# RWKV-7 recurrence: 32x32 triangular inverses by substitution on 16-blocks and 32x32 products

## The chip, the cores and the metric

The kernel runs on one core of a Trainium2 chip. The metric is the device time of one execution in microseconds (us). A core has TensorE (PE in the profile; PEld is its weight load), VectorE (DVE), ScalarE (ACT), GpSimd (POOL), SyncE (SP, which issues nearly all DMAs here) and 16 DMA engines.

## The reference

A network of four blocks on 512 tokens of width 1024 in f32: banded attention, an MLP, an RWKV-7 mixer with its MLP, and a block with an S5 and an LRU recurrence. Only the mixer's scan matters here. It runs for 16 heads of 64 channels, once forwards and once backwards over the tokens:

```python
def rwkv7_scan(r, w, k, v, kk, a):
    def step(state, inp):
        r_t, w_t, k_t, v_t, kk_t, a_t = inp
        sa = jnp.einsum('bhvk,bhk->bhv', state, -kk_t)
        state = (state * w_t[:, :, None, :] + sa[..., None] * (kk_t * a_t)[:, :, None, :]
                 + v_t[..., None] * k_t[:, :, None, :])
        return state, jnp.einsum('bhvk,bhk->bhv', state, r_t)
    ...
```

Written for a chunk of 64 tokens at a time, the steps inside a chunk become products with the inverse of a 64x64 triangular matrix with ones on its diagonal, and only the state is carried from chunk to chunk.

## The kernel before

The mixer's projections come first, then the recurrence, then the output projection. The recurrence works on 8 pairs of heads, `p` = 0 to 7. A pair has 8 chunks of 64 tokens, 2 directions `d` and 2 heads `hp`, so 32 triangular 64x64 matrices. Each is made of two 32x32 triangular blocks on the diagonal and one full block beside them. A pair therefore has 64 triangular 32x32 blocks; `g` = 2d + half numbers the four kinds, `x` = 0 to 15 the sixteen blocks of a kind (chunk and head).

Ten streams of instructions are written as Python generators, each run for p = 0 to 7:

- `front` and `half` (one per direction) load and form the decay-scaled operands `ar` and `bk` of a pair, mostly on DVE and ACT.
- `scores` multiplies them on PE, masks the products on DVE into the tile `at`, four tiles `at` a pair, and stores the triangular blocks to the DRAM scratch `nd_s`. Blocks of direction 1 are transposed on DVE first (line 1627).
- `inverse` loads a pair's 64 blocks back, so that a partition holds a whole 32x32 block (`N`). Each block stands on two partitions, one for the even rows of its inverse (`X`), one for the odd. Then 30 columns are eliminated one after the other, each by a product and a sum on DVE (lines 1656 and 1659, which the profile shows under the helper's line 1298), and `X` goes to the DRAM scratch `xd_s`.
- `early` makes `uv` from v. `merge` loads the inverses as 32x32 blocks on partitions (`yz`), transposes them on DVE (line 1700), and joins two 32-blocks into a 64-block by two rounds of 32 products of 32x32 on PE (lines 1715 and 1725), into the tile `tt`.
- `mid` multiplies with `tt` and makes, for each chunk, the matrix `m` by which the state changes. `chain` carries the state: 8 steps a pair, each a product on PE into `cp` and four ACT instructions that write the next state `ss` (line 1831). `post` normalises, and its end must be issued before the chain of the next pair begins.

The function `weave` merges the streams into one order for each engine: at every turn it takes the stream whose next instruction could start first by a model of costs and waits (2.2 us for any DMA), and of several with the same start the one whose operands were ready first. This order is fixed in the program, so an instruction that waits holds up all that stands behind it on its engine. Conditions keep the streams together. `scores` of a pair may go on only when the chain of two pairs earlier has made enough steps, because nine tiles `at` are there:

```python
yield lambda: min(done["side", 0], done["side", 1]) > 2 * p + i // 2 and done["step"] >= 2 * (4 * p + i - 9) + 2
```

`inverse` starts when the fourth tile `at` of its pair is there, `merge` when `inverse` and `early` are.

Of the kernel before, what the change touches and what calls it, by code (L numbers as in the profile page):

```python
# [24 lines left out]
class Net:  # L25
# [200 lines left out]
    def bank(self):  # L226
        return self.ps.tile([128, 512], F32, name="mm", tag="mm")
# [1063 lines left out]
    def rwkv(self, g_pre, mu_p, mu_n, w_r, w_k, w_v, w_o, k_k, k_a, r_k, gn_w, gn_b, w0, w1, w2, a0, a1, a2,  # L1291
# [4 lines left out]
        nc, tc = self.nc, self.tc  # L1296
        V, G = nc.vector, nc.gpsimd
# [29 lines left out]
        with ExitStack() as c0:  # L1327
            prm = self.pool(c0, "rprm", side="right")

            with ExitStack() as c1:  # L1330
# [3 lines left out]
                for n, lst in enumerate(((("mp", mu_p, 48), ("mn", mu_n, 48)),  # L1334
# [4 lines left out]
                    o = 0  # L1339
# [93 lines left out]
            with ExitStack() as c1:  # L1433
# [34 lines left out]

                selr = sh.tile([128, 16], F32, name="selr")
# [132 lines left out]
                def scores(p, st):  # L1602


                    nt_ = T2("nt", 1)[:, :S].rearrange("p (a b) -> p a b", b=32)
                    for i in range(4):
# [36 lines left out]
                def inverse(p, st):  # L1643

                    yield lambda: done["pre"] > p
                    N = sh.tile([128, 32, 32], F32, name="N", tag="N")
                    X = sh.tile([128, 16, 32], F32, name="X", tag="X")
# [3 lines left out]
                    yield DV, N, X  # L1651
                    xt = sh.tile([128, 240], F32, name="xt_", tag="xt_")
                    for j in range(1, 31):
                        m, n = (j + 1) // 2, 31 - j
                        t = xt[:, :m * n].rearrange("p (i c) -> p i c", c=n)
                        TT(V, t, X[:, 0:m, j].unsqueeze(2).to_broadcast([128, m, n]),
                           N[:, j, j + 1:32].unsqueeze(1).to_broadcast([128, m, n]), M)
                        yield DV, xt
                        TT(V, X[:, 0:m, j + 1:32], X[:, 0:m, j + 1:32], t, AD)
# [28 lines left out]
                def merge(p, st):  # L1688

                    yield lambda: done["inverse"] > p and done["early"] > p  # L1690
                    yz = sh.tile([128, 32, 32], F32, name="yz", tag="yz")
                    yb, zb = yz[:, 0:16], yz[:, 16:32]
                    t3 = tts[p % 2].rearrange("p c h t -> p (c h) t")
                    for g in (2, 3, 0, 1):
                        s_ = xd_d[p, 16 * g:16 * g + 16].rearrange("x (s t) -> s x t", t=32)
# [11 lines left out]
                    mx, rsb = yb, zb  # L1707
                    b = bank().rearrange("p (x t) -> p x t", t=32)
                    for i in range(4):
                        if i % 2 == 0:  # L1710
                            yield PE, st["at", i], mx
                        for x in range(4 * i, 4 * i + 4):
                            for d in range(2):
                                o = 32 + 32 * d
                                MM(b[Q((1, 2)[d] if x % 2 else 3 * d), x, :], st["at", i][Q(3 * d), x // 2 % 2, x % 2, 2 * d, o:o + 32], mx[Q(3 * d), x, :], True, True)
# [5 lines left out]
                    for x in range(16):  # L1721
                        if x % 8 == 0:
                            yield PE, rsb, mx
                        for d in range(2):
                            MM(b[Q(1 + d if x % 2 else 3 * d), x, :], rsb[Q(1 + d), x, :], mx[Q(1 + d), x, :], True, True)
# [337 lines left out]
```

## Time and profile before

| what | value |
|---|---|
| median of 3 runs | 2375.42 us (2374.48 to 2377.2) |
| the profiled execution | 2374.26 us, its span 2372.5 us |
| PE busy | 2148.4 us (91%), 14218 instructions |
| DVE busy | 1350.9 us (57%), 2862 instructions |
| ACT busy | 1084.0 us (46%), 1958 instructions |
| recurrence, from its first masked scores to its last state | 872 to 1376 us of the span |
| in it: PE, DVE, ACT busy | 400.37, 353.61, 322.46 us of 504 |
| in it: mean granted clock of PE | 0.83 of full speed |

The shares of the whole span mix the recurrence with projections in which PE is busy nearly all the time. What the change is worth has to be read from the recurrence alone. The profiled execution is 1.2 us below the median; 1.8 us of it lie outside the span.

### The profile page before, as it was taken

The page shows a single profiled execution, that of the slowest core. Times are in us where ns is not written, and L with a number is a line of the kernel's source. Part 1 is how long each engine was busy: PE and PEld are TensorE (multiplying, and loading weights), DVE is VectorE, ACT ScalarE, POOL GpSimd, SP SyncE. Part 2 cuts the span into 40 slices and gives each one's busy share as a digit, 9 for nine tenths or more (in the row PEclk, how much of TensorE's full clock was granted, in tenths as well). Part 3 has the DMA queues.
Part 4 walks back from the last instruction along what each step waited for, and adds up shares of the span by engine and source line. Part 5 has one row for each costly group of instructions (what it writes and reads, how often), then busy time and mean ns, then how long its engine had stood idle before and what let it go on. Part 6 is the DMA issues. An engine that isn't in the chain of part 4 may idle for free. (4 is left out here: it accounts for less than half of the span.)

```text
span 2372.5 us, 36431 instructions
## 1 busy us (share of the span) xinstructions
PE 2148.4 (91%) x14218; PEld 1737.5 (73%) x14218; DVE 1350.9 (57%) x2862; ACT 1084.0 (46%) x1958; POOL 82.7 (3%) x121
## 2 busy tenths in 40 slices
PE   8998999999978965788888779999999999999998
PEld 6777788888756854667666658888787877788877
DVE  4556542333479568487867446287655657732353
ACT  4555353342356454567665645342333444532232
POOL 0000000000000001011111000000000000000000
PEclk9999999999979985788889989999999989899999
DMA  5311233233332423233323153234244454233341
GB/s 170 102 54 53 80 107 92 86 107 97 99 103 63 146 65 74 43 65 67 75 44 72 49 173 105 89 109 124 97 134 128 143 133 115 66 90 100 104 142 54
DMA packets 352375, 226.54 MB, mean 95 GB/s; under 512 B 114799, under 2 KB 306315, under 8 KB 352203
## 3 DMA queue, kind: packets, MB, share of 16 engines
q1 hardware_dynamic: 350762, 218.97, 32.8%
q10 hardware_dynamic: 1440, 5.24, 0.6%
q8 instruction: 112, 1.84, 0.3%
q14 instruction: 61, 0.49, 0.1%
HBM read 193.94 MB, written 27.07 MB: 93 GB/s over the span
## 5 line engine op out<-in xcount | busy, mean ns | idle before, releaser
L160 ACT ACTIVATE whi<-raw 128x1024 fp32r<-128x1024 f32 x228 | 239.6, 1052 | 603.0 <-PE mm L223 318.2
L161 DVE TENSOR_TENSOR wlo<-raw,whi 128x1024 fp32r<-128x1024 f32 x228 | 276.3, 1214 | 385.8 <-ACT whi L160 383.0
L222 PE MATMUL mm<-uth,whi 128*128 128x512 f32 (+1 forms) x1088 | 411.7, 380 | 1.7 <-ACT uth L196 1.7
L223 PE MATMUL mm<-utl,whi 128*128 128x512 f32 (+1 forms) x1088 | 406.0, 374 | 5.3 <-DVE utl L197 5.3
L224 PE MATMUL mm<-uth,wlo 128*128 128x512 f32 (+1 forms) x1088 | 406.2, 374 | 0.0
L223 PEld LDWEIGHTS mm<-utl,whi 128*128 128x128 f32 x1088 | 208.1, 191 | 42.9 <-DVE utl L197 6.6
L222 PEld LDWEIGHTS mm<-uth,whi 128*128 128x128 f32 x1088 | 207.8, 192 | 40.5 <-ACT uth L196 2.9
L224 PEld LDWEIGHTS mm<-uth,wlo 128*128 128x128 f32 x1088 | 208.0, 191 | 37.1 <-issue 1.1
L224 PE MATMUL mm<-whi,hl 128*128 128x512 f32 x512 | 200.6, 394 | 0.0
L222 PE MATMUL mm<-whi,hh 128*128 128x512 f32 x512 | 200.5, 394 | 0.0
L223 PE MATMUL mm<-wlo,hh 128*128 128x512 f32 x512 | 199.9, 393 | 0.0
L224 PEld LDWEIGHTS mm<-whi,hl 128*128 128x128 f32 x512 | 96.3, 188 | 22.0 <-issue 0.2
L223 PEld LDWEIGHTS mm<-wlo,hh 128*128 128x128 f32 x512 | 96.3, 188 | 21.7
L222 PEld LDWEIGHTS mm<-whi,hh 128*128 128x128 f32 x512 | 96.3, 188 | 21.4 <-issue 0.4
L1302 PE MATMUL mb<-ar,bk 64*128 64x128 f32 x512 | 85.4, 330 | 16.1 <-DVE ar L1298 13.8
L223 PE MATMUL mm<-mx,whi 128*128 128x512 f32 x224 | 91.3, 407 | 4.5 <-DVE mx L1289 4.4
L222 PE MATMUL mm<-whi,uth 128*128 128x512 f32 x224 | 88.5, 401 | 6.7 <-ACT whi L160 6.4
L222 PE MATMUL mm<-mx,whi 128*128 128x512 f32 x224 | 87.3, 410 | 7.2 <-ACT mx L1288 6.2
L1302 PEld LDWEIGHTS mb<-ar,bk 64*128 64x128 f32 x512 | 72.6, 227 | 24.6 <-issue 15.5
L224 PE MATMUL mm<-mx,wlo 128*128 128x512 f32 x224 | 90.0, 402 | 0.0
L224 PE MATMUL mm<-whi,utl 128*128 128x512 f32 x224 | 88.5, 398 | 0.0
L223 PE MATMUL mm<-wlo,uth 128*128 128x512 f32 x224 | 88.0, 396 | 0.0
(534 smaller groups left out, 3887.9 us busy)
## 6 DMA issues: line engine op xcount, KB each, us to landing
raw<-in_mlp_w_dram SPq DMA_DIRECT2D x128, 512.0 KB, 4.1
raw<-in_w_in_dram SPq DMA_DIRECT2D x44, 512.0 KB, 3.8
raw<-in_attn_w_in_dram SPq DMA_DIRECT2D x18, 512.0 KB, 4.2
gbt<-in_norm_g_dram ACTq DMA_DIRECT2D x8, 512.0 KB
raw<-in_attn_w_out_dram SPq DMA_DIRECT2D x8, 512.0 KB
raw<-in_rk_w_k_dram SPq DMA_DIRECT2D x8, 512.0 KB, 4.4
h_s<-h SPq DMA_DIRECT2D x8, 512.0 KB, 2.7
raw<-in_rk_w_v_dram SPq DMA_DIRECT2D x8, 512.0 KB
```

Of the source, the lines that this page charges most:

```text
L160: nc.scalar.activation(out=hi[:, :n], in_=raw[:, :n], func=AF.Copy)
L161: nc.vector.tensor_tensor(out=lo[:, :n], in0=raw[:, :n], in1=hi[:, :n].bitcast(F32), op=ALU.subtract)
L222: mm(out, lhsT=lhs[0], rhs=rhs[0], start=start, stop=False)
L223: mm(out, lhsT=lhs[0], rhs=rhs[1], start=False, stop=False)
L224: mm(out, lhsT=lhs[1], rhs=rhs[0], start=False, stop=stop)
L1302: MM = lambda o, l, r, a, b: nc.tensor.matmul(o, lhsT=l, rhs=r, start=a, stop=b)
```

## The change

`inverse` no longer eliminates 30 columns of a 32x32 block. A partition now holds one of the two 16x16 triangular blocks on the diagonal of a 32-block: 64 blocks of 32 make 128 of 16, one to a partition, and 14 columns are eliminated in place in `X`. Direction 1 comes in untransposed (`XL`), and one DVE copy turns it round inside each partition. `merge` loads these inverses as 32x32 blocks with zeros beside the diagonal (`yd`), transposes them (`zd`), and makes the 32-blocks on PE: 64 products of 32x32, a mask on DVE (`v1`, with the constant `off`), then 4 products of 32x512 with the identity and 64 products of 32x32 summed on them. From there on it goes as before, except that the operands lie the other way round, which drops two ACT copies.

```diff
+                X, XL, yd, zd = (sh.tile([128, 16, 32], F32, name=n) for n in ("X", "XL", "yd", "zd"))
+                for t in (X, XL, yd):
+                    G.memset(t, 0.0)
...
 def scores(p, st):
-                        yield DV, at
                         for g in (2, 3, 0, 1):
-                            d = g // 2
-                            e = 64 * d + 32 * (g % 2)
-                            s_ = at[Q(g), :, :, 2 * d, e:e + 32].rearrange("p j h t -> p (j h) t")
-                            if g >= 2:
-                                V.transpose(out=nt_[Q(g), 4 * i:4 * i + 4], in_=s_)
-                                s_ = nt_[Q(g), 4 * i:4 * i + 4]
+                            s_ = at[Q(g), :, :, 2 * (g // 2), diag(g)].rearrange("p j h t -> p (j h) t")
...
 def inverse(p, st):
-                    for e in range(2):
-                        nc.sync.dma_start(out=N[H(e)].rearrange("p a b -> p (a b)"), in_=nd_d[p])
-                        nc.sync.dma_start(out=X[H(e)], in_=nd_d[p].rearrange("x (i e t) -> x i e t", e=2, t=32)[:, :, e, :])
+                    for q in range(2):
+                        for d in range(2):
+                            o = slice(64 * d + 32 * q, 64 * d + 32 * q + 32)
+                            nc.sync.dma_start(out=flat((X, XL)[d][o])[:, :512 - 16 * q], in_=nd_d[p, 32 * d:32 * d + 32, 528 * q:512 + 512 * q])
+                    yield DV, XL
+                    V.tensor_copy(out=X[H(1), :, 0:16], in_=XL[H(1), :, 0:16].rearrange("p s t -> p t s"))
...
-                    for j in range(1, 31):
-                        m, n = (j + 1) // 2, 31 - j
+                    for j in range(1, 15):
+                        n = 15 - j
...
-                    for e in range(2):
-                        V.memset(flat(X[H(e)])[:, e:512:34], 1.0)
-                        nc.sync.dma_start(out=xd_d[p].rearrange("x (i e t) -> x i e t", e=2, t=32)[:, :, e, :], in_=X[H(e)])
+                    V.memset(flat(X)[:, 0:512:33], 1.0)
+                    nc.sync.dma_start(out=xd_v[p], in_=flat(X))
...
 def merge(p, st):
-                        nc.sync.dma_start(out=yb[Q(g)], in_=s_)
-                        if g < 2:
-                            nc.sync.dma_start(out=t3[Q(g), :, 32 * g:32 * g + 32], in_=s_)
-                    yield DV, yz
-                    V.transpose(out=zb, in_=yb)
-                    for q in range(2):
-                        nc.sync.dma_start(out=t3[Q(2 + q), :, 32 * q:32 + 32 * q], in_=zb[Q(2 + q)])
-                    for q in range(2):
-                        yield AC, yz
-                        ACT(yb[Q(2 * q)], zb[Q(2 * q)], AF.Copy)
+                        for q in range(2):
+                            r = 64 * (g // 2) + 32 * q + 16 * (g % 2)
+                            nc.sync.dma_start(out=yd[32 * g + 16 * q:32 * g + 16 * q + 16, :, 16 * q:16 * q + 16],
+                                              in_=xd_v[p, r:r + 16].rearrange("x (s t) -> s x t", t=32)[:, :, 0:16])
+                    yield DV, yd
+                    V.transpose(out=zd, in_=yd)
...
+                                MM(b[Q(g), x, :], st["at", i][Q(g), x // 2 % 2, x % 2, 2 * (g // 2), diag(g)], by[g][Q(g), x, :], True, True)
+                    yield DV, b
+                    v1 = sh.tile([128, 16, 32], F32, name="v1", tag="v1")
+                    TT(V, v1, b, off.unsqueeze(1).to_broadcast([128, 16, 32]), M)
+                    yield PE, v1
+                    b = bank().rearrange("p (x t) -> p x t", t=32)
+                    for g in range(4):
+                        MM(b[Q(g)], self.ident[Q(g), Q(g)], of[g][Q(g)], True, False)
+                    for x in range(16):
+                        for g in range(4):
+                            MM(b[Q(g), x, :], v1[Q(g), x, :], of[g][Q(g), x, :], False, x == 15)
...
+                    yield AC, b
+                    ACT(yb, b, AF.Copy)
+                    yield DV, yz
+                    V.transpose(out=zb, in_=yb)
+                    for g in range(4):
+                        nc.sync.dma_start(out=t3[Q(g), :, 32 * (g % 2):32 * (g % 2) + 32], in_=yb[Q(g)])
```

Since `weave` sets the order from its costs, other streams move too. On DVE, in the inverse of the first pair, before (`xt_` holds the products, line 1298 is the helper for two tensors, lines 1300 and 1550 belong to `half` of the next pairs):

```order
L1298 TENSOR_TENSOR xt__6800<-X,N 128x54
L1300 TENSOR_SCALAR tmp<-tmp 128x8x64
L1298 TENSOR_TENSOR X<-X,xt__6800 128x2x27
L1298 TENSOR_TENSOR xt__6800<-X,N 128x78
L1300 TENSOR_SCALAR tmp<-tmp 128x8x64
L1550 SCALAR_TENSOR_TENSOR tmp<-cm,tmp 128x520
L1298 TENSOR_TENSOR X<-X,xt__6800 128x3x26
L1550 SCALAR_TENSOR_TENSOR tmp<-cm,tmp 128x520
```

The same place in the changed kernel:

```order
L1660 COPY X<-XL 64x16x16
L1298 TENSOR_TENSOR xt__6783<-X 128x14
L1298 TENSOR_TENSOR X<-X,xt__6783 128x14
L1298 TENSOR_TENSOR xt__6783<-X 128x26
L1300 TENSOR_SCALAR tmp<-tmp 128x8x64
L1298 TENSOR_TENSOR X<-X,xt__6783 128x2x13
L1298 TENSOR_TENSOR xt__6783<-X 128x36
L1298 TENSOR_TENSOR X<-X,xt__6783 128x3x12
```

Between the first and the last of the 60 instructions of this inverse stood 51 rows of other streams; between the first and the last of the 28 stand 5.

On DVE, at the end of that inverse before (line 1700 is the transpose in `merge`):

```order
L1298 TENSOR_TENSOR xt__6800<-X,N 128x15
L1298 TENSOR_TENSOR X<-X,xt__6800 128x15
L1662 MEMSET X 64x16 x2
L1700 STREAM_TRANSPOSE yz<-yz 128x512
L1298 TENSOR_TENSOR xt__7259<-X,N 128x30
```

In the changed kernel 25 rows of other streams stand between the end of this inverse and the first transpose of its merge (`zd`), and the second transpose (line 1733) stands behind the whole inverse of the second pair:

```order
L1298 TENSOR_TENSOR xt__7127<-X 128x14
L1298 TENSOR_TENSOR X<-X,xt__7127 128x14
L1671 MEMSET X 128x16
L1300 TENSOR_SCALAR rn<-mb 128x8
L1733 STREAM_TRANSPOSE yz<-yz 128x512
```

So the transpose that stood directly behind the inverse has moved away from it.

On DVE, around the merge of the fifth pair (p = 4), before; 24 rows stand between this transpose and the end of its inverse:

```order
L1862 TENSOR_REDUCE rg<-tmp 128x8
L1599 COPY bns<-mb 128x8
L1298 TENSOR_TENSOR at<-mb,mk 128x2x2x128
L1700 STREAM_TRANSPOSE yz<-yz 128x512
L1300 TENSOR_SCALAR rg<-rg 128x16
L1599 COPY bns<-mb 128x8
L1298 TENSOR_TENSOR xt__10233<-X,N 128x30
```

and in the changed kernel, where the row `MEMSET X` ends the inverse of the pair:

```order
L1671 MEMSET X 128x16
L1298 TENSOR_TENSOR at<-mb,mk 128x2x2x128
L1298 TENSOR_TENSOR tmp<-mb,v 128x512 x2
L1298 TENSOR_TENSOR m<-mb,ar_8101 128x2x64
L1298 TENSOR_TENSOR m<-mb,ar_8109 128x2x64
L1298 TENSOR_TENSOR m<-mb,ident_6292 128x2x128
L1298 TENSOR_TENSOR at<-mb,mk 128x2x2x128
L1707 STREAM_TRANSPOSE zd<-yd 128x512
L1298 TENSOR_TENSOR at<-mb,mk 128x2x2x128
L1298 TENSOR_TENSOR v_10462<-mb,off 128x512
```

The merge here stands beside the chain of the pair before (rows `m` and `at`), behind its own inverse by seven instructions.

## Rows read from the trace of the kernel before

**Rows 1.** Stretches: us, busy PE, PEld, DVE, ACT, POOL (instructions), clock, DMA share, GB/s

```profile
872.00:968.20 96.20, 58.57 (x682) 48.95 (x683) 76.40 (x219) 45.45 (x87) 9.12 (x13) 0.62 0.33 70
968.20:1035.10 66.90, 57.26 (x852) 46.32 (x848) 41.25 (x132) 42.66 (x108) 6.49 (x6) 0.87 0.23 45
1035.10:1098.50 63.40, 54.76 (x667) 42.65 (x667) 54.39 (x161) 42.46 (x103) 6.55 (x6) 0.73 0.31 68
1098.50:1153.80 55.30, 47.81 (x761) 38.44 (x762) 37.84 (x113) 43.33 (x110) 6.60 (x6) 0.94 0.31 64
1153.80:1212.20 58.40, 46.19 (x651) 35.94 (x653) 49.75 (x151) 38.88 (x97) 6.53 (x6) 0.85 0.32 65
1212.20:1266.00 53.80, 50.06 (x792) 41.04 (x788) 38.34 (x129) 34.07 (x95) 4.79 (x3) 0.90 0.26 51
1266.00:1313.10 47.10, 35.36 (x505) 27.78 (x506) 34.45 (x110) 28.60 (x80) 4.73 (x3) 0.93 0.36 73
1313.10:1354.80 41.70, 33.29 (x606) 26.53 (x601) 16.11 (x55) 28.72 (x82) 2.89 (x1) 0.96 0.13 21
```

**Rows 2.** Timeline, ACT: first state of pairs 0 and 1 (start, us, operation)

```profile
968.18 1.31 ACT L1301 ACTIVATE ss<-cp,wc 64x64 f32<-64x64 f32 x4
...
1035.11 1.29 ACT L1301 ACTIVATE ss<-cp,wc 64x64 f32<-64x64 f32 x4
```

**Rows 3.** Timeline, DVE and PE: inverse and merge of pair 0; [idle before, releaser]

```profile
901.80 0.19 DVE L1298 TENSOR_TENSOR xt__6800<-X,N 128x30 f32<-128x30 f32 x1 [1.87 <-DMA X<-nd_s]
...
945.71 0.18 DVE L1298 TENSOR_TENSOR X<-X,xt__6800 128x15 f32<-128x15 f32 x1
...
955.52 0.71 DVE L1700 STREAM_TRANSPOSE yz<-yz 128x512 f32<-128x512 f32 x1 [9.46 <-DMA yz<-xd_s]
...
956.94 1.08 PE L1302 MATMUL mb<-yz,at 32*32 32x32 f32 x64 [15.66 <-ACT yz L1301]
```

**Rows 4.** Groups, DVE, 872 to 1376: one inverse's 60 instructions; busy, mean ns | idle

```profile
L1298 DVE TENSOR_TENSOR xt__6800<-X,N 128x110 f32<-128x110 f32 (+20 forms) x30 | 7.4, 247 | 2.6 <-DMA X<-nd_s 1.9
L1298 DVE TENSOR_TENSOR X<-X,xt__6800 128x110 f32<-128x110 f32 (+20 forms) x30 | 7.4, 247 | 0.7
```

**Rows 5.** Groups, DVE and ACT, 872 to 1376: other instructions of scores, merge and mid

```profile
L1298 DVE TENSOR_TENSOR at<-mb,mk 128x512 f32<-128x512 f32 x63 | 42.7, 687 | 33.1 <-PE mb L1302 32.6
L1627 DVE STREAM_TRANSPOSE tmp<-at 32x128 f32<-32x128 f32 x64 | 19.5, 305 | 2.0
L1301 ACT ACTIVATE ax<-mb 128x512 f32<-128x512 f32 x32 | 19.1, 597 | 1.1 <-PE mb L1302 0.4
L1301 ACT ACTIVATE yz<-yz 32x512 f32<-32x512 f32 x16 | 10.0, 627 | 31.8 <-DVE yz L1700 28.7 <-DVE bns L1599 2.9
L1700 DVE STREAM_TRANSPOSE yz<-yz 128x512 f32<-128x512 f32 x8 | 5.7, 710 | 30.7 <-DMA yz<-xd_s 30.7
```

**Rows 6.** Timeline, DVE: two sizes of the inverse of pair 1, start to start

```profile
958.73 0.22 DVE L1298 TENSOR_TENSOR xt__7259<-X,N 128x56 f32<-128x56 f32 x1
958.99 0.22 DVE L1298 TENSOR_TENSOR X<-X,xt__7259 128x56 f32<-128x56 f32 x1
```

**Rows 7.** Timeline, PE at full clock: products of three shapes (two records each)

```profile
1115.68 0.69 PE L1302 MATMUL cp<-uv,at 128*64 128x64 f32 x16
...
1118.63 0.75 PE L1302 MATMUL mb<-yz,at 32*32 32x32 f32 x64 [0.74 <-ACT yz L1301]
...
1262.25 1.02 PE L1302 MATMUL mb<-lg,wg 128*128 128x512 f32 x2
```

**Rows 8.** DMA issues, 860 to 1376: KB each, median us from issue to landing

```profile
v<-rkv_s SPq DMA_DIRECT2D x14, 256.0 KB, 2.8
X<-nd_s SPq DMA_DIRECT2D x16, 128.0 KB, 5.5
...
yz<-xd_s SPq DMA_DIRECT2D x32, 64.0 KB, 2.9
```

More of the change, by code (lines that the diff above doesn't have):

```diff
@@ L1467, in rwkv @@
                 done["side", 0] = done["side", 1] = 0
+                X, XL, yd, zd = (sh.tile([128, 16, 32], F32, name=n) for n in ("X", "XL", "yd", "zd"))
+                for t in (X, XL, yd):
+                    G.memset(t, 0.0)
+                diag = lambda g: slice(64 * (g // 2) + 32 * (g % 2), 64 * (g // 2) + 32 * (g % 2) + 32)
+                xd_v = xd_d.rearrange("w a (b c) -> w (a b) c", c=512)
+                ind = sh.tile([128, 2], F32, name="ind")
+                V.tensor_reduce(out=ind, in_=self.ident.rearrange("p (g q c) -> p q g c", q=2, c=16), axis=AX.XY, op=AD)
+                off = sh.tile([128, 32], F32, name="off")
+                V.memset(off, 0.0)
+                for d in range(2):
+                    o = off[H(d), 16 * d:16 * d + 16]
+                    TS(V, o, o, ind[H(d), 1 - d:2 - d], None, AD, BY)
                 selr = sh.tile([128, 16], F32, name="selr")
@@ L1602, in scores @@
                 def scores(p, st):
-                    nt_ = T2("nt", 1)[:, :S].rearrange("p (a b) -> p a b", b=32)
                     for i in range(4):
@@ L1653, in inverse @@
-                    for j in range(1, 31):
-                        m, n = (j + 1) // 2, 31 - j
-                        t = xt[:, :m * n].rearrange("p (i c) -> p i c", c=n)
-                        TT(V, t, X[:, 0:m, j].unsqueeze(2).to_broadcast([128, m, n]),
-                           N[:, j, j + 1:32].unsqueeze(1).to_broadcast([128, m, n]), M)
+                    for q in range(2):
+                        for d in range(2):
+                            o = slice(64 * d + 32 * q, 64 * d + 32 * q + 32)
+                            nc.sync.dma_start(out=flat((X, XL)[d][o])[:, :512 - 16 * q], in_=nd_d[p, 32 * d:32 * d + 32, 528 * q:512 + 512 * q])
@@ new lines, in inverse @@
+                    yield DV, XL
+                    V.tensor_copy(out=X[H(1), :, 0:16], in_=XL[H(1), :, 0:16].rearrange("p s t -> p t s"))
+                    yield DV, X
+                    xt = sh.tile([128, 64], F32, name="xt_", tag="xt_")
+                    for j in range(1, 15):
+                        n = 15 - j
+                        t = xt[:, :j * n].rearrange("p (i c) -> p i c", c=n)
+                        TT(V, t, X[:, 0:j, j].unsqueeze(2).to_broadcast([128, j, n]),
+                           X[:, j, j + 1:16].unsqueeze(1).to_broadcast([128, j, n]), M)
@@ L1658, in inverse @@
                         yield DV, xt
-                        TT(V, X[:, 0:m, j + 1:32], X[:, 0:m, j + 1:32], t, AD)
+                        TT(V, X[:, 0:j, j + 1:16], X[:, 0:j, j + 1:16], t, AD)
                         yield DV, X
-                    for e in range(2):
-                        V.memset(flat(X[H(e)])[:, e:512:34], 1.0)
-                        nc.sync.dma_start(out=xd_d[p].rearrange("x (i e t) -> x i e t", e=2, t=32)[:, :, e, :], in_=X[H(e)])
+                    V.memset(flat(X)[:, 0:512:33], 1.0)
@@ L1690, in merge @@
                     yield lambda: done["inverse"] > p and done["early"] > p
[L1691 to L1692 removed]
                     t3 = tts[p % 2].rearrange("p c h t -> p (c h) t")
                     for g in (2, 3, 0, 1):
[L1695 to L1707 removed]
+                        for q in range(2):
[4 more added lines that the diff above has]
+                    V.transpose(out=zd, in_=yd)
+                    of = (yd, yd, zd, zd)
+                    by = (zd, zd, yd, yd)
                     b = bank().rearrange("p (x t) -> p x t", t=32)
@@ L1710, in merge @@
                         if i % 2 == 0:
-                            yield PE, st["at", i], mx
+                            yield PE, st["at", i], zd
+                        for x in range(4 * i, 4 * i + 4):
+                            for g in range(4):
[10 more added lines that the diff above has]
+                            MM(b[Q(g), x, :], v1[Q(g), x, :], of[g][Q(g), x, :], False, x == 15)
+                    yz = sh.tile([128, 32, 32], F32, name="yz", tag="yz")
+                    yb, zb = yz[:, 0:16], yz[:, 16:32]
+                    yield AC, b
+                    ACT(yb, b, AF.Copy)
+                    yield DV, yz
+                    V.transpose(out=zb, in_=yb)
+                    for g in range(4):
+                        nc.sync.dma_start(out=t3[Q(g), :, 32 * (g % 2):32 * (g % 2) + 32], in_=yb[Q(g)])
+                    rsb = v1
+                    b = bank().rearrange("p (x t) -> p x t", t=32)
+                    for i in range(4):
+                        if i % 2 == 0:
+                            yield PE, st["at", i], yz
                         for x in range(4 * i, 4 * i + 4):
@@ L1714, in merge @@
                                 o = 32 + 32 * d
-                                MM(b[Q((1, 2)[d] if x % 2 else 3 * d), x, :], st["at", i][Q(3 * d), x // 2 % 2, x % 2, 2 * d, o:o + 32], mx[Q(3 * d), x, :], True, True)
+                                MM(b[Q((1, 2)[d] if x % 2 else 3 * d), x, :], st["at", i][Q(3 * d), x // 2 % 2, x % 2, 2 * d, o:o + 32], zb[Q(3 * d), x, :], True, True)
                     for d in range(2):
@@ L1722, in merge @@
                         if x % 8 == 0:
-                            yield PE, rsb, mx
+                            yield PE, rsb, yz
                         for d in range(2):
-                            MM(b[Q(1 + d if x % 2 else 3 * d), x, :], rsb[Q(1 + d), x, :], mx[Q(1 + d), x, :], True, True)
+                            MM(b[Q(1 + d if x % 2 else 3 * d), x, :], rsb[Q(1 + d), x, :], yb[Q(1 + d), x, :], True, True)
                     for d in range(2):
```

4 lines of the change are left out of this document (removed).

## The prediction

> **What bounds the kernel now.** I read the table of stretches first, then DVE's and PE's timelines around the first merge, then the groups by cost, then the DMA issues. The stretches are cut where each pair writes its first state [rows 1, 2], so a row is one period of the recurrence. The reader is to see three things there. The first row, 96.2 us up to the first state, has DVE busy for 76.4 and PE at a mean clock of 0.62: DVE paces the start. The next five rows last 66.9 to 53.8 us, with PE busy for 46 to 57 of them. So PE comes first in a running period, but it works at a mean clock of 0.73 to 0.94. The clock has two levels, 2.4 GHz and 1.2; the mean of a stretch tells how long it stood on the lower. The periods alternate: 63.4 and 58.4 us with clock 0.73 and 0.85, then 55.3 and 53.8 with 0.94 and 0.90. In the long ones the inverse ends late and PE has too little to do. In the last two rows no scores are left, and a period takes 47.1 and 41.7 us.
>
> The first merge shows the mechanism [rows 3]. Its inverse runs on DVE from 901.80 to 945.71, 44 us. Then DVE idles 9.46 us until the inverses have come back through DRAM, and PE's first merge product has 15.66 us of idle time in front of it. The 60 instructions themselves are 14.8 us busy [rows 4]; the rest of the 44 is other streams' work in between.
>
> **The change, part by part.**
>
> *Removed from DVE, for each pair.* The 60 instructions, 14.8 us [rows 4], and 8 transposes in `scores` of 0.305 us, 2.4 us [rows 5].
>
> *Added to DVE.* 28 instructions of 14 to 56 elements. The largest takes 0.22 us [rows 6], 15 and 30 elements take 0.18 and 0.19 [rows 3]. I take 0.205, 5.7 us; the bounds are 5.0 and 7.3 (28 times 0.18 and, start to start, 0.26). The copy that turns direction 1 round, 256 elements on half the partitions, no row shows: between 0.18 and the 0.69 of 512 elements [rows 3, 5] I take half of the latter, 0.35, for its count. The mask `v1` costs what the masked scores cost, 0.69, and the second transpose 0.71 [rows 5]. Net: -17.2 + 5.7 + 0.35 + 0.69 + 0.71 = -9.8 us of DVE a pair, 78 us in all. That is no time saved by itself, only where DVE paces.
>
> *ACT.* Two copies of 0.627 go, one of 512 elements comes, 0.597 [rows 5]: -0.66 us, costed at nothing, since PE and the waits of the chain cover it.
>
> *Added to PE, for each pair.* Two rounds of 64 products of 32x32, 128 records each, and 4 products of 512 columns with the identity. The old round of 64 records lasts 0.75 us, 11.7 ns a record; 16 records of 64 columns over all rows last 0.69, 43 ns each, so 21.6 ns would be the share of 32 columns [rows 7]. The old round is thus about twice as fast as one product after the other, with two row groups in use. The new rounds use four. Bounds for one new round: 0.75 us if all four go side by side, 2.8 if they take turns (128 times 21.6 ns). I take 1.5, the old pace a record, because it is the nearest row. A product of 512 columns over all rows takes 1.02 us with its two records [rows 7]; the four take 1.0 us side by side and 4.1 in turn; I take 1.0, as they lie on four different row and column groups. Sum 4.0 us at full clock, bounds 2.5 and 9.7.
>
> The Trainium skill, page "TensorEngine Tiling (Array Packing)", section "Gotcha 1: PSUM Pressure", says that different row tiles cannot access the same PSUM bank at the same time. All four row groups of a new round write one bank, so by it the sum would be the upper bound, 9.7. The row speaks against it: the old round also writes one bank from two row groups, and is twice as fast as turns.
>
> *DMAs.* A load of 256 KB in long rows lands after 2.8 us, the old loads of `X` and stores in 128-byte pieces after 5.5 [rows 8]. The new loads of `X`, `XL` and the store are long rows: about 2.7 us less each way. The loads of `yd` are 8 of 64-byte pieces instead of 4 of 128: their landing I put at 2.9 as for `yz` [rows 8], the bounds are 1.5 and 5.8 (half and double). Eight issues instead of four or six on SP cost it about a microsecond more; nothing but the next score stores is queued behind. Together the way from the end of an inverse to its transpose stays near today's 9.6 us (from 945.71 + 0.18 to 955.52) [rows 3], say 8 to 9.
>
> *The start.* Up to the first state DVE loses 9.1 (the first inverse, 14.8 - 5.7) and 2.4 (the transposes of the second pair's scores), less 0.35 for the copy: -11.1. The 9.46 us in which DVE idled now lie under 25 rows of other work: -9.5. Added are `v1` and a transpose, +1.4, and the inverse of the second pair, +6.1, which now stands ahead of the second transpose. PE's new products run at the same time as that inverse. Sum -13 us.
>
> *The first period, 66.9 us.* It holds the second pair's inverse and merge, which now lie before it; so it becomes a running period.
>
> *A running period.* Clock times busy PE gives 40.0, 44.9, 39.3 and 45.1 us of work at full clock in the rows of 63.4 to 53.8 us [rows 1], 42.3 in the mean. With the 4.0 it is 46.3. The inverse is off the path now: the merge stands beside the chain of the pair before, in every period alike. So I take the clock of the two short periods, 0.92, and a little less than their idle time of PE (7.5 and 3.7): 5.0. 46.3 / 0.92 + 5.0 = 55.3 us. The four middle periods go from 230.9 us to 221.2, -9.7; the first from 66.9 to 55.3, -11.6.
>
> *The end.* In the row of 47.1 us PE idles for 11.7, and its merge is late; I take -4 there, and +2 for the added products in the last two pairs, together -2. What is late next, everywhere, is PE itself and DVE's wait for `yd`.
>
> Sum: -13 - 11.6 - 9.7 - 2 = -36.3. The profiled execution took 2374.3 us (span 2372.5 and 1.8 around it), so 2338; the median of the runs stands 1.1 above it: 2339 us.
>
> **The rivals.**
>
> *The round through DRAM was the pace, not PE.* `scores` of a pair waits for the chain of two pairs before; if that loop sets the period, each microsecond off the inverse counts, and PE then idles little: 46.3 / 0.92 = 50.3 us a period, -30 in the four, -16.6 in the first, -19 at the start (-13 with the second pair's 6.1 us hidden too), -4 at the end: 2374 - 70 = 2304, 2305 against the median. For it: the periods alternate, and PE idles in the long ones. Against it: PE is busy 86% of those five periods. Chance 0.18.
>
> *The rows of tiles take turns.* Then 5.7 us more of PE a pair, 6.2 at clock 0.92: five periods and two at the end, 31 and 6: 2338 + 37 = 2375, no change. This is the time by the skill's rule. Against it stands the old round's pace [rows 7]. Chance 0.08.
>
> *DVE stands at the new transpose (the other side).* It follows its inverse by seven instructions, some 4 us, where `weave` counts 2.2 us for a DMA and two of them take 8 to 9. Everything behind it on DVE waits, the masks of scores and `m` among it, for which PE and the chain wait, and PE's clock falls as in the row of 63.4 us. Today this wait is 30.7 us over the pairs [rows 5], but in half of them the transpose stands far behind the inverse. If each period becomes like that row: start -13 + 9.5, first -3.5, middle +22.7, end +6: +22, 2397. It decides from a period of 62.6 us on, where the sum is zero. For it: the 9.46 us of the first pair [rows 3]. Against it: rows around it are work that DVE has to do anyway, and PE has chain and scores to go on with. Chance 0.12.
>
> **How the numbers follow.** A measurement of this kernel can tell about 0.2%, 4.7 us, from no change. The forecast has 0.62. Faster by more: 0.62 + 0.18 = 0.80. Of the turns 0.06 are within it and 0.02 slower; the late transpose is slower: 0.14. The range goes down to 2300, under the first rival, and up to 2378, which takes in the turns with the upper bound of PE's price; it leaves out the late transpose and the far end of the first rival.
>
> **What would show it.** In the changed kernel DVE's busy time should be 75 to 80 us less and the 28 instructions of an inverse near 5.7 us; PE's new rounds near 1.5 us each, the four wide products near 1.0; the first state near 955 us; the middle periods near 55 us and alike. If the idle time before `zd` is over 60 us in sum, or a new round takes 2.8 us, the forecast is wrong by the rival named; periods near 50 us would say that PE never was the pace.

## The result, and the profile after

The changed kernel takes 2347.49 us (median of 4 runs, 2344.52 to 2348.09), the kernel before 2374.95 on the same chip (4 runs): ratio 0.9883, 95% interval 0.9865 to 0.9900. That is 27.5 us faster; 36 were forecast, and the time lies in the range. The profiled execution took 2344.52 us, its span 2342.3.

The stretches of the changed kernel, cut where each pair writes its first state, answer to [rows 1]:

```profile
872.00:959.70 87.70, 66.18 (x1221) 53.56 (x1222) 66.45 (x172) 45.47 (x86) 9.05 (x13) 0.70 0.30 69
959.70:1016.80 57.10, 53.78 (x845) 43.23 (x841) 30.84 (x93) 39.12 (x104) 6.54 (x6) 0.91 0.14 30
1016.80:1067.40 50.60, 44.76 (x909) 35.73 (x907) 35.69 (x96) 40.50 (x100) 6.83 (x6) 0.97 0.27 64
1067.40:1119.80 52.40, 48.57 (x996) 38.70 (x995) 36.98 (x103) 41.16 (x104) 6.84 (x6) 1.00 0.26 63
1119.80:1173.30 53.50, 48.75 (x996) 38.78 (x995) 36.93 (x103) 41.14 (x103) 6.83 (x6) 1.00 0.23 57
1173.30:1234.30 61.00, 57.08 (x968) 46.32 (x967) 34.29 (x103) 32.63 (x92) 4.80 (x3) 0.80 0.19 41
1234.30:1283.90 49.60, 44.48 (x906) 36.08 (x906) 21.89 (x66) 32.44 (x90) 4.80 (x3) 0.97 0.20 44
1283.90:1327.70 43.80, 37.20 (x784) 29.25 (x785) 13.51 (x31) 25.78 (x73) 2.89 (x1) 0.84 0.15 33
```

The periods no longer alternate, DVE's share is down (36.9 us busy of 52 to 54, where it had 38 to 54), and in two of the five PE runs at its upper clock (1.00 is 2.4 GHz) all the time and idles for 4 to 5 us only. The start is 8.5 us shorter, the five running periods 23.2 (297.8 to 274.6), the end 4.6 longer. The part behind the last state, in which nothing is changed, is 3.1 shorter.

DVE's groups from 872 to 1376 answer to [rows 4] and [rows 5]:

```profile
L1733 DVE STREAM_TRANSPOSE yz<-yz 128x512 f32<-128x512 f32 x8 | 5.7, 711 | 25.7 <-ACT yz L1301 25.6
L1707 DVE STREAM_TRANSPOSE zd<-yd 128x512 f32<-128x512 f32 x8 | 5.7, 709 | 7.2 <-DMA yd<-xd_s 7.1
L1298 DVE TENSOR_TENSOR v<-mb,off 128x512 f32<-128x512 f32 x8 | 5.5, 690 | 19.7 <-PE mb L1302 19.7
L1660 DVE COPY X<-XL 64x256 f32<-64x256 f32 x8 | 3.1, 386 | 0.3
L1298 DVE TENSOR_TENSOR X<-X,xt__6783 128x14 f32<-128x14 f32 (+6 forms) x14 | 2.8, 201 | 0.4
L1298 DVE TENSOR_TENSOR xt__6783<-X 128x14 f32<-128x14 f32 (+6 forms) x14 | 2.8, 199 | 0.4
```

Two rows of 14 instructions at 0.20 us are an inverse: 5.6 us, as forecast. The wait of the first transpose is 7.1 us over all pairs and not over 60, so DVE does not stand at `zd`. Its new waits lie behind, for PE (19.7) and ACT (25.6), in a stretch in which it has time.

PE in a running period, timeline: first and last row of the first round, what follows it, the wide products, first and last row of the second round, and what follows:

```profile
1086.87 0.22 PE L1302 MATMUL mb<-zd,at 32*32 32x32 f32 x2
...
1087.95 0.21 PE L1302 MATMUL mb<-yd,at 32*32 32x32 f32 x2
1088.09 1.09 PE L1302 MATMUL mb<-at,ta 128*64 128x128 f32 x16
...
1089.75 0.62 PE L1302 MATMUL mb<-yd,ident 32*32 32x512 f32 x2
...
1090.64 0.19 PE L1302 MATMUL mb<-yd,v 32*32 32x32 f32 x2
...
1091.86 0.21 PE L1302 MATMUL mb<-zd,v 32*32 32x32 f32 x2
1092.00 1.16 PE L1302 MATMUL mb<-ar,bk 64*128 64x128 f32 x8
```

From start to the next thing a round takes 1.22 us. The wide products take 0.89 (1089.75 to 1090.64). The second round took 1.36 here and 1.20 where nothing interrupted it.

What the forecast did not have are gaps of PE put down to issue, that is, with nothing to wait for. The waits of PE's products, 872 to 1376, of the changed kernel (us in total, times, longest); the kernel before has no such row for its products (PE's weight loads, which overlap the products, have such rows in both):

```profile
PE mb L1302 <- issue: 7.2, 7, 2.5
```

### The profile page after: what moved, and what is told of

Same layout as the page of the kernel before. It is cut to its first block, busy times and chain, and to the rows that moved or that the text cites. A ratio compares the mean times of both kernels' runs of the same rounds, so it can differ in the third digit from the quotient of the medians.

```text
span 2342.3 us, 40343 instructions
## 1 busy us (share of the span) xinstructions
PE 2158.5 (92%) x16330; PEld 1745.3 (75%) x16330; DVE 1279.1 (55%) x2562; ACT 1078.4 (46%) x1950; POOL 84.9 (4%) x124
## 5 line engine op out<-in xcount | busy, mean ns | idle before, releaser
L224 PEld LDWEIGHTS mm<-uth,wlo 128*128 128x128 f32 x1088 | 208.1, 191 | 36.9 <-issue 1.1
L1301 ACT ACTIVATE ss<-cp,wc 64x64 f32<-64x64 f32 x224 | 69.1, 309 | 36.8 <-PE cp L1302 31.5
```

The source lines that it names most:

```text
L224: mm(out, lhsT=lhs[1], rhs=rhs[0], start=False, stop=stop)
L1301: ACT = lambda o, i, f, **k: nc.scalar.activation(out=o, in_=i, func=f, **k)
```

## The experiments

Each ratio is to the kernel before, run beside it on the same chip. The same kernel can still differ by several us: the changed kernel measured again on another chip (`c1`) has ratio 0.9844. Also, the part behind the last state, the same code in all kernels, lasted from 995.7 to 1006.2 us, and a ratio contains it. So the table sets apart the start (first state), the five periods from the first state of pair 0 to that of pair 5, and the rest to the last state, from the profiled executions in us.

| kernel | ratio to before (95%) | first state | five periods | rest |
|---|---|---|---|---|
| before | 1 | 968.2 | 297.8 | 106.3 |
| changed | 0.9883 (0.9865 to 0.9900) | 959.7 | 274.6 | 110.9 |
| c1, changed again | 0.9844 (0.9808 to 0.9880) | 960.2 | 267.1 | 109.9 |
| e1, DVE load in inverse | 1.0034 (1.0011 to 1.0056) | 969.8 | 286.8 | 117.7 |
| e2, DVE load spread | 1.0139 (1.0095 to 1.0182) | 985.2 | 307.6 | 111.9 |
| e3, PE products twice | 1.0134 (1.0080 to 1.0189) | 971.3 | 309.5 | 129.8 |
| e4, one row group at a time | 1.0124 (1.0087 to 1.0161) | 967.2 | 311.2 | 122.7 |
| e5, spaced rounds | 1.0048 (1.0027 to 1.0070) | 965.1 | 301.9 | 114.2 |
| e6, quarter of instructions | 0.9783 (0.9762 to 0.9803) | 958.5 | 258.7 | 105.4 |
| e7, one more hop | 0.9871 (0.9850 to 0.9891) | 962.6 | 269.7 | 109.5 |
| e8, products on POOL | 0.9970 (0.9949 to 0.9990) | 961.2 | 289.3 | 109.7 |
| e9, no inverse steps | 0.9851 (0.9819 to 0.9883) | 954.7 | 270.0 | 109.7 |
| e10, short inverse in before | 0.9862 (0.9829 to 0.9896) | 949.4 | 287.0 | 103.3 |
| e11, half the load | 0.9950 (0.9929 to 0.9970) | 960.6 | 278.3 | 108.8 |

Theory P, that PE paces the changed kernel's periods, stands against D (DVE's load paces), L (the inverse's length paces) and the prediction's rival of the round through DRAM. D2, in two of the expectations, is D at half to two thirds of the load. Theory I concerns the supply of instructions. In e1 to e4, e6 to e9 and e11 the order of each engine is that of the changed kernel.

**c1.** 

> The changed kernel itself, beside the three other kernels of this group on one chip, as what they are compared with. Every theory: its ratio to the kernel before near 0.988, the gaps of PE put down to issue again inside the new rounds and about 7 us in sum.

Its second to fifth periods:

```profile
1016.50:1069.50 53.00, 47.16 (x909) 37.60 (x907) 35.73 (x96) 40.59 (x99) 6.84 (x6) 0.90 0.25 61
1069.50:1121.80 52.30, 48.44 (x996) 38.59 (x995) 37.05 (x103) 41.25 (x105) 6.84 (x6) 1.00 0.26 63
1121.80:1174.50 52.70, 48.75 (x996) 38.77 (x995) 36.95 (x103) 41.20 (x103) 6.83 (x6) 1.00 0.24 57
1174.50:1227.30 52.80, 47.28 (x968) 37.70 (x967) 34.22 (x103) 32.69 (x92) 4.81 (x3) 1.00 0.21 47
```

The period of 61.0 us at clock 0.80 above is 52.8 us here, at 1.00. The code is the same, so that loss isn't the kernel's. Whether it goes with the execution or with the chip is not shown: all four runs above took 2344 to 2348 us, three of the four here 2333 to 2337 and one 2352. So what follows is held against both. The gaps put down to issue return (6.9 us).

**e1 and e2: the DVE load put back.**

```diff
 in inverse (e1), behind each sum; in half (e2), behind seven products
+    TT(V, dum, dum, dum, M)     # 128x512
```

> Edit: 14 more DVE products of 128x512 on a tile that nothing reads, one behind each step of the inverse; the order of all other instructions is held. At about 0.68 us each this puts 9.5 us a pair back on DVE, inside the inverse, about what the change took off (9.8). Theory P (PE paces the running periods, the inverse lies off the path): the first state comes 9.5 to 19 us later, since DVE paces the start and two inverses stand ahead of it; the periods behind it stay within 1 us each; in all 10 to 22 us over the changed kernel. Theory L (the length of the inverse is what the periods wait for): the start and 5 us or more in each period, 45 us or more. Theory D (DVE's load as such): 9.5 us a pair, about 76 us.

> Edit: the same 14 DVE products of 128x512 a pair, but behind the products of the two streams that form the operands (seven for each direction), so that the inverse keeps its length and DVE's load is that of the run before; the order of all other instructions is held. Theory P: the start is 9.5 to 19 us later (the operands of two pairs are formed in it), the periods within 1 us each, in all 10 to 22 us. Theory L: only the start, and nothing in the periods, so well under the run with the load inside the inverse. Theory D: 9.5 us a pair, about 76 us.

Two running periods of e1, then two of e2:

```profile
1085.90:1141.80 55.90, 50.83 (x997) 39.83 (x995) 44.27 (x117) 41.23 (x104) 7.48 (x6) 0.97 0.24 59
1141.80:1198.50 56.70, 50.98 (x995) 40.74 (x995) 44.17 (x117) 41.15 (x103) 7.48 (x6) 0.94 0.22 53
```

```profile
1107.70:1169.20 61.50, 56.55 (x996) 45.20 (x995) 45.40 (x117) 41.33 (x104) 6.54 (x6) 0.83 0.22 54
1169.20:1230.30 61.10, 55.55 (x996) 44.35 (x995) 45.30 (x117) 41.06 (x103) 6.54 (x6) 0.86 0.21 50
```

DVE has 7 to 8 us more in these periods, and they are 3 to 4 us longer with the load in the inverse, 8 to 9 with it spread; in the mean of all five periods it is 2.4 to 3.9 and 6.6 to 8.1. PE's records are the same; it waits more and its mean clock falls from 1.00 to 0.94 and 0.83. With its DVE load put back the change gains nothing (ratios over 1). Theory P's "within 1 us" fails, and so does L: the load costs more outside the inverse than in it. D's 76 us is too much for e1 (36 to 45 us over the changed kernel, by its two ratios), and nearly reached by e2 (61 to 70). In e2 the load stands in the streams that form the operands of `scores`, so it lengthens that way too; no run sets the two apart.

**e9 and e11: less of it, and half of it.**

```diff
 inverse (e9)
-    TT(V, t, X[:, 0:j, j]..., X[:, j, j + 1:16]..., M)
-    TT(V, X[:, 0:j, j + 1:16], X[:, 0:j, j + 1:16], t, AD)
 inverse (e11), behind each sum
+    if j % 2: TT(V, dum, dum, dum, M)
```

> Edit to the changed kernel: the 28 products and sums of each inverse are left out (the blocks go through uninverted, so this part is not computed); loads, copy, store and the order of everything else are held. 5.6 us a pair off DVE. Theory D2: 6 to 11 us in the start and 2 to 3.5 in each period, 22 to 32 us faster than the changed kernel. Theory P: 6 to 11 us in the start and nothing in the periods.

> Edit to the changed kernel: 7 more DVE products of 128x512 in each inverse, where the run with the load inside the inverse had 14; the order of all else is held. 14 of them made the last state 37 us later than in the changed kernel run beside it on another chip (10 in the start, 27 in the periods); leaving the 28 steps out made the start 5.5 us earlier and the periods no shorter. If DVE paces from the changed kernel's load on (a straight line from there): half of it, 5 us in the start and 13 or 14 in the periods, about 18 us. If there is a margin (DVE idles 15 of 52 us in a period) and the loss begins behind it: the start's 5 us and 0 to 5 in the periods. If PE's clock decides and falls at the first delay: as much as with 14, 25 us or more in the periods.

The third and fourth periods of e9, then of e11:

```profile
1065.80:1117.70 51.90, 48.43 (x996) 38.59 (x995) 32.79 (x75) 41.17 (x105) 6.68 (x6) 1.00 0.26 63
1117.70:1170.30 52.60, 48.77 (x996) 38.79 (x995) 32.70 (x75) 41.12 (x103) 6.67 (x6) 1.00 0.25 58
```

```profile
1074.80:1128.90 54.10, 48.56 (x996) 38.51 (x995) 40.62 (x110) 41.14 (x103) 7.21 (x6) 1.00 0.25 61
1128.90:1183.40 54.50, 48.95 (x996) 38.70 (x995) 40.63 (x110) 41.15 (x103) 7.21 (x6) 1.00 0.23 56
```

Without the steps DVE has 4.2 us less in a period, and the period stays at 52 us: only the start gains (5.0 to 5.5 us, a little under the 6 expected), as theory P says. So the periods have a floor, and the changed kernel stands on it. That the floor is PE's follows from its clock of 1.00, its 4 us of idle time, and from e3, e4 and e6 below.

With half the load the run is 16 to 25 us over the changed kernel by the ratios, but about 7 of them lie behind the last state, where the code is the same. The start is at most 0.9 us later, where the straight line and the margin both had 5. The five periods (56.3, 57.9, 54.1, 54.5 and 55.5 us) are 3.7 us longer than the changed kernel's and 11.2 longer than `c1`'s: under the straight line's 13 or 14, and in or above the margin's 0 to 5, by which of the two it is held against. The two periods shown are 1.8 us longer than in `c1`, with PE still at clock 1.00. Between the straight line and a margin this run does not decide; with twice the load (e1, e2) the floor is left. That joins the two theories: a DVE load like that of the kernel before costs the changed kernel its gain, and with the load of the change PE paces it.

**e3 and e4: what PE's products cost.**

```diff
 merge (e3): each new round and the wide products issued twice
 merge (e4)
-    for x in ...: for g in range(4): MM(b[Q(g), x, :], ...)
+    for g in range(4): for x in ...: MM(b[Q(g), x, :], ...)
```

> Edit: both new rounds and the four wide products are issued twice, into the same banks with the same values; the order of all else is held. 264 more PE records a pair; at the paces of the changed kernel's trace (about 0.95 us a round of 128 records and 0.43 us for the wide ones, at full clock) 2.4 us a pair. Theory P: 2.4 us in each period and in the start, about 19 us in all, and nothing hidden. If PE has slack in the periods (it idles 4 to 6 us in each): 0 to 5 us. Theory I (a dense round of small products runs faster than instructions reach PE, and the gaps put down to issue, 7.2 us in the changed kernel and none before, are that): the gaps grow to 14 us or more, and the whole comes to 25 us or more.

> Edit: the same products in another order inside the two new rounds: all eight (first round) or sixteen (second round) blocks of one row group, then the next row group, so that neighbours use the same rows; nothing else moves. By the prediction's own price of turns (21.6 ns a record at full clock) a round of 128 takes 2.8 us where it takes about 0.95 now. If the four row groups do run side by side in the changed kernel, and theory P holds: 3.7 us a pair, 26 to 30 us in all, less what the gaps put down to issue give back (up to 7 us), since at the slower pace instructions keep up (theory I: no such gap over 0.5 us in the rounds). If the row groups take turns already: no change. If PE has slack in the periods: 0 to 8 us.

The expectations' 0.95 us a round was too small: it is 1.22 to the next operation. e4's second round of one pair, timeline (some records missing), and e3's and e4's waits for issue, 872 to 1420:

```profile
1240.65 1.99 PE L1306 MATMUL mb<-yd,v 32*32 32x32 f32 x61
...
1242.57 1.99 PE L1306 MATMUL mb<-zd,v 32*32 32x32 f32 x61
...
1244.49 1.86 PE L1306 MATMUL mb<-ar,bk 64*128 64x128 f32 x7
```

```profile
PE mb L1305 <- issue: 32.0, 20, 2.7
```

```profile
PE mb L1306 <- issue: 0.4, 1, 0.4
```

With neighbours on the same rows a round takes 3.84 us (1240.65 to 1244.49) and 3.46 in the first round; with the four row groups in turn 1.2. So they do run side by side, though all four write one bank: the second rival falls. The Trainium skill's page "TensorEngine Tiling (Array Packing)", section "Gotcha 1: PSUM Pressure", says they can't at the same time; the measurement decides. In both runs nothing of PE's work is hidden, as theory P says: the five periods are 35 to 44 us longer, where the added work alone is 5 x 3.3 = 17 us in e3 and 5 x 4.9 = 24 in e4. So the sizes miss: by the ratios e3 is 59 to 69 us over the changed kernel and e4 57 to 66, where P had 19 and 26 to 30. In e3 the gaps put down to issue grow from 7 to 32 us, as theory I says; in e4 all but one of 0.4 us are gone. In both the mean clock of the periods is 0.78 to 0.97, so the clock falls without such gaps too. Why it does is open.

**e6 and e5: the gaps taken away.**

```diff
 merge (e6)
-    for x in range(4 * i, 4 * i + 4): MM(b[Q(g), x, :], at[x], by[g][Q(g), x, :], True, True)
+    MM(b[Q(g), 4 * i:4 * i + 4, :], at[0], by[g][Q(g), 4 * i:4 * i + 4, :], True, True)
 merge (e5): before each further 16 products of a round
+    yield lambda: self.turns > n      # another stream has put a step on PE
```

> Edit: in the two new rounds one product of 32x128 stands for four of 32x32: the same columns go through PE with a quarter of the instructions (32 in place of 128 a pair); it leaves out three quarters of the left operands, so it is not the same computation; the order of everything else is held. By PE's work alone: a round of 128 records at 0.95 us becomes one of 32 records at about the pace of the wide products (0.45 us), 1.0 us a pair, 8 us in all. Theory I: besides these 8 the gaps put down to issue (7 us) go, and with them the half clock behind the fifth pair's first state (about 9 us): 15 to 25 us faster than the changed kernel.

> Edit: the same products, but each new round is handed out in four pieces of 16 products of 32x32, and between two pieces at least one step of another stream must have been put on PE; the order of the other streams is replanned around that. Theory I (dense rounds outrun the supply of instructions, and PE's clock falls after such gaps): the gaps put down to issue fall from 7 us to 2 or less, the stretch at half clock behind the fifth pair's first state goes, and the run is 5 to 15 us faster than the changed kernel. Without theory I: the merge only comes later, 0 to 5 us slower.

e6 has no gap of PE's products put down to issue, and is the fastest run: 11.5 us under `c1` by the medians (2324.02 and 2335.51, same chip). Its rounds take 1.01 and 0.98 us in place of 1.22 and 1.20, which is worth 0.43 x 8 = 3.4 us, and the gaps 6.9: 10.3. The first period of `c1`, then the first and the third of e6:

```profile
960.20:1016.50 56.30, 53.79 (x845) 43.47 (x841) 30.81 (x93) 39.16 (x103) 6.54 (x6) 0.91 0.14 30
```

```profile
958.50:1011.40 52.90, 49.48 (x843) 39.95 (x839) 30.78 (x93) 39.04 (x104) 6.49 (x6) 1.00 0.15 32
1063.80:1115.60 51.80, 47.85 (x803) 37.84 (x803) 36.65 (x103) 41.22 (x103) 6.84 (x6) 1.00 0.26 63
```

The third period, in which `c1` has no gap, is 0.5 us shorter, about the 0.43 of the rounds; the fifth, in which `c1` has 2.2 us of gaps, is 3.1 shorter. The half-clock stretch that the expectation named, behind the fifth pair's first state, is not in `c1` and could not go. The first period is 3.4 us shorter by its clock (0.91 and 1.00); it holds no merge, so the edit's part in that is not shown. e5 has no such gap either, but is 51 us slower than `c1` by the medians, and both its expectations miss (5 to 15 faster, 0 to 5 slower): its order was planned anew, and the periods alternate between 69 and 51 us. It says nothing on the gaps.

**e7: one more hop on the way through DRAM.**

```diff
-    nc.sync.dma_start(out=xd_v[p], in_=flat(X))
+    nc.sync.dma_start(out=flat(XL), in_=flat(X))
+    nc.sync.dma_start(out=xd_v[p], in_=flat(XL))
```

> Edit: the inverses go through one more transfer of 256 KB (from X to the idle half-used tile XL, and from there to DRAM), 2.5 to 3 us longer on the way from an inverse to its first transpose; the order of all engines is held. If the round through DRAM sets the period (the first rival of the prediction): 2.5 to 3 us in each period and two of them in the start, 20 us or more. Theory P (PE paces, the way through DRAM is covered): DVE stands 2 to 3 us longer at the first transpose, the periods grow by less than 1 us each, the start by up to 3: 3 to 9 us in all. If every delay of DVE reaches PE and its clock, as the runs with more DVE work suggest: 2 us or more a period, 15 us or more.

The wait of DVE at the first transpose, in `c1` and then in e7:

```profile
L1707 DVE STREAM_TRANSPOSE zd<-yd 128x512 f32<-128x512 f32 x8 | 5.7, 710 | 6.1 <-DMA yd<-xd_s 5.7 <-issue 0.4
```

```profile
L1719 DVE STREAM_TRANSPOSE zd<-yd 128x512 f32<-128x512 f32 x8 | 5.7, 710 | 21.8 <-DMA yd<-xd_s 16.6 <-DMA nd_s<-at 5.2
```

So the hop reaches DVE, 2.0 us a pair. The start is 2.4 us longer than in `c1`, the five periods 2.6, half a microsecond each, as theory P says. The first rival falls for the changed kernel; in the kernel before it was not tested. The median is 11 us over `c1`'s; 8.8 of the profiled executions' difference lies behind the last state, where the code is the same.

**e8: DVE products moved to POOL.**

```diff
-    TT(V, kd, r, kd, M)
+    TT(G, kd, r, kd, M)      # and two more forms, five instructions a pair
```

> Edit to the changed kernel: five SBUF products of 128x512 a pair (0.68 us each on DVE) are done by POOL in their places, 3.4 us a pair off DVE; the order of all engines is held. Theory D2 (what is taken off DVE comes back as time at half to two thirds, since every delay of DVE reaches PE and its clock, as the two runs with added DVE work say): 13 to 18 us faster than the changed kernel. Theory P (DVE is covered in the periods): only the start, 3 to 7 us faster. A third way: POOL takes so long for such a product that the operands come late: slower by any amount, and the products' rows show it.

Slower than the change. POOL and DVE at one place of it:

```profile
1051.09 2.06 POOL L1300 TENSOR_TENSOR tmp<-r,tmp 128x512 f32<-128x512 f32 x1 [27.45 <-DVE bk L1300]
...
1055.67 1.31 POOL L1300 TENSOR_TENSOR tmp<-r,tmp 128x512 f32<-128x512 f32 x1 [0.63 <-DVE bk L1300]
```

```profile
1052.04 3.03 DVE L1612 COPY wc<-tmp 64x8 f32<-64x8 f32 x2
...
1055.77 1.49 DVE L1300 TENSOR_TENSOR bk<-tmp 128x256 f32<-128x256 f32 x1
...
1057.52 0.34 DVE L1612 COPY wc<-tmp 64x8 f32<-64x8 f32 x2
```

A POOL product takes 1.3 to 2.1 us where DVE took 0.68, and while it runs some DVE instructions stand: two copies take 3.03 us beside it and 0.34 alone, a product of 256 columns 1.49 beside it and 0.42 elsewhere. The Trainium skill's page "SBUF — State Buffer", section "SBUF: two separate sides", describes this: a pair of ports that DVE and GpSimd share and lock for a whole instruction. The trace agrees. Neither theory is tested by this run.

**e10: the short inverse in the kernel before.**

```diff
-    for j in range(1, 31):
+    for j in range(1, 15):      # and half the width
```

> Edit to the kernel before the change: its loop runs over 14 columns of half the width and not over 30, so DVE has the 28 short instructions of the changed kernel (9.1 us a pair less), and PE has none of the new products; the rest of the inverse is left out. The order is replanned. If DVE's relief makes the whole gain and PE's added products take some of it back: faster than the changed kernel by the 8 to 15 us that the run with a quarter of the instructions won or more, ratio to the kernel before 0.975 to 0.98. If the gain came from the place that the merge got in the order (beside the chain of the pair before): the periods go on alternating and the ratio stays above 0.99.

No better than the change, with none of its products on PE. The first state comes 10 us earlier than in the change, but the order was planned anew, and its periods alternate (56.5, 51.8, 61.5, 50.5 and 66.7 us). Both expectations miss, the ratio of the first (0.975 to 0.98) and that of the second (above 0.99): the relief of DVE alone makes the same gain. That the less regular order costs here what the products on PE cost in the change is argued and not shown.

## Why the prediction was right, and where its sizes were off

- *DVE's work.* The terms came out: 5.6 us an inverse, copy 0.39, mask 0.69, transpose 0.71. The busy time of the whole, which counts overlap once, fell by 71.8 us (1350.9 to 1279.1), just short of the 75 to 80 named.
- *"That is no time saved by itself, only where DVE paces."* True of the changed kernel (e9), and too mild for the kernel before: there the relief of DVE makes the gain by itself (e10), and the load put back on the changed kernel takes the gain away, through PE's waits and clock (e1, e2).
- *PE's products, 4.0 us a pair.* 1.22 + 1.20 + 0.89 = 3.3, and 7.2 / 8 = 0.9 of gaps put down to issue: 4.2. The sum was right by luck: the rounds and the wide products were cheaper, and the gaps were not in the forecast.
- *The DMAs.* The loads of `yd` landed after 1.9 us in the median, not 2.9. The 5.5 us that the prediction gives for the old loads and stores is, in [rows 8], that of the loads of `X` alone.
- *The start, -13: measured -8.5.* In `c1` -8.0. The step that failed is "PE's new products run at the same time as that inverse". For the first pair they do. The second transpose comes 16.8 us earlier than the transpose before (938.76 against 955.52), but the first state follows it after 21.0 us, not 12.7: the second pair's rounds stand ahead of the chain's first product on PE, 949.67 to 953.91 and 954.93 to 958.47, the first with a gap of 2.5 us for issue in it, the second at half the clock (the wide products take 1.71 us there, not 0.89). Timeline, DVE's row and then PE's:

```profile
938.76 0.71 DVE L1733 STREAM_TRANSPOSE yz<-yz 128x512 f32<-128x512 f32 x1
```

```profile
949.67 0.22 PE L1302 MATMUL mb<-zd,at 32*32 32x32 f32 x2
...
953.72 0.18 PE L1302 MATMUL mb<-yd,at 32*32 32x32 f32 x1 [2.50 <-issue]
...
954.93 1.06 PE L1302 MATMUL mb<-yd,ident 32*32 32x512 f32 x2
...
958.47 0.69 PE L1302 MATMUL cp<-uv,at 128*64 128x64 f32 x16
```

- *The first period, -11.6: -9.9, in `c1` -10.6.* It became no running period: it holds no merge, and its clock is 0.91.
- *The four middle ones, -9.7: -13.3, in `c1` -20.1.* Clock times busy PE, in the mean of the four rows, is 46.6 us (`c1` 46.7) against the 46.3 forecast, and PE idles 4.6 (`c1` 4.8) against 5.0. The term that was mis-sized is the clock: 0.92 forecast, 0.94 in this execution with its period at 0.80, and 0.975 in `c1`.
- *The end, -2: +4.6, in `c1` +3.6.* The 4 us for a merge no longer late came: PE's idle time in the row of 47.1 us falls from 11.7 to 5.1 (`c1` 4.7). The step that failed is the +2 for the added products: in the two stretches behind the fifth period PE's busy time rises from 68.7 us [rows 1] to 81.7 (`c1` 78.2), or, times the clock, from 65 to 74 and 75. The rounds and wide products of two merges are 6.6 us of these 10, and little other work is left to cover them.
- *Sum.* -8.5 - 9.9 - 13.3 + 4.6 = -27.1, and -2.6 outside (behind the last state and beside the span) make the 29.7 between the profiled executions. In `c1` the sum is -8.0 - 10.6 - 20.1 + 3.6 = -35.1 against -36.3. That it comes so near is in part luck: start and end were taken 10.6 us too well, the periods 9.4 too badly.
- *The rivals.* The DRAM round (e7), the turns (e4) and the wait at `zd` (7.1 us) all fell. The third rival's 62.6 us, from where its sum is zero, holds with the forecast's own start and end; with the rival's (-3.5 and +6) it is 59.1.

Open is why PE's clock fell in the fifth period of one execution and not in `c1`: in both, two gaps put down to issue, 1.0 to 1.6 us from start to start, lie ahead of the place.

## What to carry to other kernels

Relief of an engine is worth its time only down to the floor of the next one. Add work to it and take work from it, with the order held: here 4 us less on DVE gave nothing in a period, and 7 to 8 more cost 2 to 8 in the mean of five. Spread small PE products over row groups in turn, and count their instructions as well as their time.

## What was not expected of the hardware

PE's instructions arrive in blocks, through a queue of their own, and a dense round outruns them. The pages' row of that queue (packets, MB, share), of the kernel before, the changed one and e3:

```profile
q8 instruction: 112, 1.84, 0.3%
```

```profile
q8 instruction: 129, 2.11, 0.4%
```

```profile
q8 instruction: 145, 2.38, 0.4%
```

The change adds 2112 records of products and as many weight loads to PE, and 17 packets of 16 KB: 4224 / 17 = 248 instructions a packet. All of PE's instructions give the same, 2 x 16330 / 129 = 253, so the queue is PE's. In the trace's DMA records of the recurrence these packets never start closer together than 3.3 us (3.5 in the changed kernel, 3.4 in `c1`, 3.3 in e3), about 75 instructions a microsecond, while a round issues 256 in 1.2 us. Every gap of over 0.5 us of PE's products that is put down to issue there, in both executions of the changed kernel and in e3, ends 1.2 to 1.6 us after such a packet has landed. Two of those rows of the changed kernel, behind packets that landed at 1196.67 and 1200.19:

```profile
1198.07 0.22 PE L1302 MATMUL mb<-zd,at 32*32 32x32 f32 x2 [1.32 <-issue]
...
1201.74 0.22 PE L1302 MATMUL mb<-zd,v 32*32 32x32 f32 x2 [0.85 <-issue]
```

The Trainium skill's page "Runtime: NRT & Kernel Launch", section "Instruction fetch mechanics", gives the blocks (256 instructions) and says that the fetch is hidden because instructions are dispatched more slowly. The packets agree; the 7.2 and 32.0 us of gaps show that it isn't hidden for such rounds.
